# Sample attention of a two-layer decoder step: value products moved next to the following logits, a third key-page buffer, and a later start

## The chip, the core and the metric

The kernel runs on one core of a Trainium2 chip. The metric is device time in microseconds (us) for one launch, from start to end of the program; lower is better. A profiled execution has two times: the device time of that execution, and its span, which runs from the first to the last recorded instruction. Engines are named as in the profile: PE is TensorE's matmul side, PEld its weight loads, DVE is VectorE, ACT is ScalarE, POOL is GpSimd and SP is SyncE, whose queue (SPq) issues all the transfers spoken of here.

## What is computed

One inference step of a two-layer decoder trunk, for a prompt of 1024 tokens and for eight sample sequences of eight tokens each. Layer 0 mixes tokens with gated linear attention. Layer 1 is stick-breaking attention, and the change touches only the sample part of it. Cut to what matters:

```python
def sb_attend(q, k, v, bias, q_offset):
    # z = q.k/sqrt(dh) + bias_h ; key s is read by query t iff s < t
    z = einsum('bqhd,bkhd->bhqk', qi, k) * dh**-0.5 + bias
    valid = k_pos < q_pos
    rest = cumsum(where(valid, log_sigmoid(-z), 0), axis=keys, reverse=True)
    a = exp(where(valid, z + rest, -inf))
    return einsum('bhqk,bkhd->bqhd', a, v)

# samples: 256 past positions in two pages of 128, found through page_table
k_past = gather_pages(cache_k, page_table)      # (8, 256, 16 heads, 64)
v_past = gather_pages(cache_v, page_table)
ys = (sb_attend(q, concat(k_past, k), concat(v_past, v), bias, 256) * silu(g)) @ w_out
```

A page of keys or values of all 16 heads is 128 x 1024 float32, 512 KB; each of the eight sequences reads two of each, so this stage loads 16 MB in 32 transfers.

## The kernel before

The whole kernel is one function. It does not issue its work in the order of its text: every piece is registered with `at(time, function, ...)` and the pieces are then run in the order of these due times. The unit is a *step*: one output tile of a dense product, 24 matmuls of 512 columns in `dense` (helper line L293, where the tile is called acc). The PE engine is the only one whose instructions are kept in exactly this order (`ENGINES` on line 41, `manual_schedule` on line 91). The order of DVE, ACT, POOL and of SP's queue comes from a planner that takes the due order as priority and its own estimate of when things are ready. Each of these queues is executed in order: an instruction that waits holds up all that are behind it.

The end of the program looks like this. `last` is the due time at which prompt attention is over. The output product of layer 1 (16 dense steps for the prompt, two shorter ones for the samples) began about 5.5 steps ahead of `last`; 15 prompt steps come first, then the two sample steps, then the last prompt step. The attention of the eight sample sequences lies between these dense matmuls: its small pieces are put between them on PE, one sequence every `EVERY` = 0.8 of a step. A sequence b has the base time s0 = last + 0.3 + 0.8 b, and its pieces in order are:

- `load_k` (line 1090, due s0 - 0.25): reads the two page numbers into registers and issues the two key pages (L1095) into kp, a tile of two buffers.
- `turn_k` (line 1104, due s0 + 0.5, 0.6, 0.7 and 0.8): four groups of four PE transposes (L1107) that turn the key pages into a bank called tr; ACT copies groups 1 and 3 to KT (L1110), DVE groups 2 and 4 (L1112). There are two tr banks, used in turn by everything that transposes.
- `spread_q` (line 1114, due s0 + 0.6): DVE copies of the queries into QB (L1117).
- `logits_s` (line 1120, due s0 + 1.2): 16 matmuls onto strips of 32 rows of the bank z (L1125), one for the mask (L1127), then two sigmoids on ACT (L1129, L1130).
- `load_v` (line 1098, due s0 + 1.25): issues the two value pages (L1102) into vp, two buffers.
- `stick_s` (line 1132, due s0 + 1.5): a DVE scan (L1135) and a multiply (L1137), which leaves the weights in As.
- `turn_s` (line 1139, due s0 + 1.85): three transposes of As (L1142, L1143), copied by ACT (L1146) and DVE (L1147).
- `weigh_s` (line 1149, due s0 + 2.15): the value products, 24 matmuls onto strips of 32 rows of the bank o (L1154: 16 with the pages vp, 8 with the new rows vs), then two DVE operations (L1157, L1160).
- `turn_o` (line 1162, due s0 + 2.5): one transpose (L1164), copied by DVE (L1166) and then ACT (L1167) into oTs.

When the last sequence is done, `gate_s` (line 1169, due s1 = s0 + 2.75) multiplies by the gate and writes hs (L1170 to L1172), which the first sample matmul needs; it is due at s1 + `S_GAP` at the earliest (line 1201). The residual of a dense step comes from memory into xr (L719), is added on DVE (L725), and goes out (L728).

Of the kernel before, what the change touches and what calls it, by code (L numbers as in the profile page):

```python
# [9 lines left out]
F32 = mybir.dt.float32  # L10
# [7 lines left out]
D = 1024  # L18
# [25 lines left out]
class Timeline:  # L44
# [8 lines left out]
    def at(self, time, fn, *args):  # L53
        assert time >= self.now, (time, self.now)
        heapq.heappush(self.heap, (time, self.n, fn, args))
        self.n += 1
# [20 lines left out]
def tile_hybrid_decoder(ctx, tc, x_prompt, x_sample, state_gla, cache_k, cache_v, page_table,  # L77
# [28 lines left out]

    C_SC, C_T, C_TS = 0.6, 0.9, 2.1
    UNIT0, PACE, L_STICK, L_TURN, L_AV = 1.45, 0.42, 0.26, 0.8, 1.3
    EVERY, S_GAP, TAIL = 0.8, 0.5, 1

    XRING = 3
    NX = {'mid': 3, 'at1': 2, 'sa': 3}
# [3 lines left out]
    at = line.at  # L116
# [11 lines left out]
    def sb(pool, name, shape, dtype=F32, bufs=2, tag=None):  # L128
        return pools[pool].tile(shape, dtype, name=name, tag=tag or name, bufs=bufs)
# [532 lines left out]
    for h in range(GH):  # L662
# [3 lines left out]
        for c, (c_0, n) in enumerate(CH):  # L666
            st = {}
            G.append(st)
            if h == 0:
                a, b = QK0[c]  # L670
                la = LA0[c]
            else:
                a, b = i, i + 1
# [5 lines left out]
            for j, (key, out) in enumerate((("q", q_out), ("k", k_out))):  # L679
                lo, hi = a + (b - a) * 0.5 * j, a + (b - a) * 0.5 * (j + 1)  # L680
                dense_t(lo, hi, c_0, n, wqk,
                        lambda w, k, j=j: (w[k // 2], slice((k % 2) * 256 + j * 128, (k % 2) * 256 + j * 128 + 128)),
# [306 lines left out]
    for p in range(PAIRS):  # L989
# [27 lines left out]
        for m in range(NP // 2):  # L1017
# [10 lines left out]
            for x, (j, c) in enumerate(units):  # L1028
                u = {}
# [14 lines left out]
    last = z0 + L_AV + 0.4  # L1044
# [45 lines left out]
    def load_k(u, b):  # L1090
        u["r"], u["k"] = [], []
        for j in range(2):
            r = nc.sync.value_load(Z["pts"][0:1, 2 * b + j:2 * b + j + 1], min_val=0, max_val=n_phys - 1)
            u["k"].append(sb("sa", "kp", [128, D]))
            nc.sync.dma_start(u["k"][j], ck[bass.ds(r, 1)].rearrange("o p f -> (o p) f"))  # L1095
            u["r"].append(r)

# [75 lines left out]

    at(last, sa_consts)
    for b in range(NB):
        u, s0 = {}, last + 0.3 + EVERY * b
        at(s0 - 0.25, load_k, u, b)
        for j in range(2):
            for g in range(2):
                at(s0 + 0.5 + 0.2 * j + 0.1 * g, turn_k, u, j, g)  # L1180
        at(s0 + 0.6, spread_q, b)
        at(s0 + 1.2, logits_s, u, b)
        at(s0 + 1.25, load_v, u)
        at(s0 + 1.5, stick_s, u)
        at(s0 + 1.85, turn_s, u)
        at(s0 + 2.15, weigh_s, u, b)
        at(s0 + 2.5, turn_o, u, b)
    s1 = s0 + 2.75
    at(s1, gate_s)


# [55 lines left out]
```

## Time and profile before

| | us |
|---|---|
| median of three runs | 1372.65 (1367.76 to 1372.90) |
| the profiled execution, device time | 1375.27 |
| its span | 1373.6 |
| PE busy in the span | 1282.8 (93%) |
| DVE busy | 1012.5 (74%) |
| ACT busy | 709.7 (52%) |
| POOL busy | 587.0 (43%) |
| mean granted clock of PE, as a share of full speed | 0.986 |

PE busy is the sum of the times in which at least one matmul was in the engine; matmuls overlap, so this is not a measure of how well the array is used. Timeline times count from the start of the span. In a timeline row the bracket at the end gives the time for which the engine had been idle before this row, and what released it.

### The profile page before, as it was taken

To read this page: it belongs to the slowest core of one execution; us is meant where nothing else is said; L and a number is where in the kernel's file an instruction comes from. 1 tells how busy PE (TensorE), PEld (TensorE's weight loads), DVE (VectorE), ACT (ScalarE), POOL (GpSimd) and SP (SyncE) were. 2 spreads that over 40 slices of the span, in tenths; PEclk is the share of its full clock that TensorE was granted. 3 is DMA by queue.
4 is the path that set the end of the run, shared out by engine and by line. 5 is a ranking of instruction groups with operands and counts; after the bars stand their busy time and mean duration, and the time that the engine had idled before them with its cause. 6 is when DMAs were issued, how large, how long until landed. Compare 5 with 4: busy or idle time off the path is not lost.

```text
span 1373.6 us, 23656 instructions
## 1 busy us (share of the span) xinstructions
PE 1282.8 (93%) x8025; PEld 1140.3 (83%) x8025; DVE 1012.5 (74%) x2047; ACT 709.7 (52%) x1640; POOL 587.0 (43%) x1101
## 2 busy tenths in 40 slices
PE   6999999999999998989989899898998989989998
PEld 5788888888878788989889898898998988877666
DVE  7858759668564457788888988789788898986443
ACT  6446245352441134566756667566666667763221
POOL 6223223223231216465655846557466574543000
PEclk9999999999999999999999999999999999999999
DMA  6311402304246423020110201102012022134762
GB/s 195 92 32 43 137 20 68 108 32 133 91 129 213 145 101 104 18 81 18 58 42 22 79 17 55 47 24 80 16 41 63 23 89 68 32 121 155 249 245 88
DMA packets 118459, 115.82 MB, mean 84 GB/s; under 512 B 11003, under 2 KB 97923, under 8 KB 118339
## 3 DMA queue, kind: packets, MB, share of 16 engines
q1 hardware_dynamic: 118338, 114.31, 27.2%
q8 instruction: 64, 1.05, 0.3%
q14 instruction: 57, 0.46, 0.1%
HBM read 83.61 MB, written 30.67 MB: 83 GB/s over the span
## 4 chain that ended last, share of the span: by engine, by line
PE 55%; DVE 18%; POOL 9%; ACT 7%; issue 7%; DMA 3%; SPq 1%; POOLq 0%; ACTq 0%; DVEq 0%
PE acc L293 31%; PE acc L315 7%; DVE run L908 4%; PE z L881 3%; PE tr L932 3%; PE o L944 2%; POOL wlo L222 2%; POOL rs L804 2%; ACT qh L853 2%; DVE whi L221 2%; PE o L544 1%; DVE aT L935 1%; DVE wr L217 1%; POOL v L819 1%; PE o L1154 1%
## 5 line engine op out<-in xcount | busy, mean ns | idle before, releaser
L293 PE MATMUL acc<-whi,h 128*128 128x512 f32 (+1 forms) x1728 | 538.7, 374 | 10.1 <-DVE qk L810 7.9
L293 PEld LDWEIGHTS acc<-whi,h 128*128 128x128 f32 x1728 | 313.5, 189 | 41.1 <-ACT sh L954 4.2
L293 PE MATMUL acc<-wlo,h 128*128 128x512 f32 (+1 forms) x864 | 322.5, 373 | 3.9 <-DVE wlo L222 2.5
L315 PE MATMUL acc<-h,whi 128*128 128x256 f32 (+5 forms) x832 | 193.5, 318 | 10.3 <-DVE g L512 5.1
L222 POOL TENSOR_TENSOR wlo<-wr,whi 128x512 fp32r<-128x512 f32 x98 | 139.1, 1422 | 123.5 <-DVE whi L221 93.2
L293 PEld LDWEIGHTS acc<-wlo,h 128*128 128x128 f32 x864 | 162.8, 188 | 22.7 <-DVE wlo L222 3.2
L908 DVE TENSOR_TENSOR_SCAN run<-om,run 128x256 f32<-128x256 f32 x192 | 146.7, 802 | 11.0 <-ACT om L884 10.5
L315 PEld LDWEIGHTS acc<-h,whi 128*128 128x128 f32 (+2 forms) x832 | 141.3, 189 | 15.1 <-DVE g L512 6.0
L934 ACT ACTIVATE aT<-tr 128x512 fp32r<-128x512 f32 (+1 forms) x160 | 88.9, 556 | 103.9 <-PE tr L932 90.2
L884 ACT ACTIVATE om<-z,bias 128x512 f32<-128x512 f32 (+1 forms) x160 | 103.3, 646 | 52.6 <-PE z L881 43.1
L932 PE MATMUL tr<-ident,A 128*128 128x128 f32 x576 | 91.5, 277 | 39.3 <-POOL v L819 18.3
L315 PE MATMUL acc<-h,wlo 128*128 128x256 f32 (+2 forms) x392 | 123.8, 316 | 0.5 <-POOL wlo L222 0.5
L293 PE MATMUL acc<-w,h 128*128 128x384 f32 (+1 forms) x480 | 122.6, 365 | 0.7 <-DVE qk L810 0.7
L932 PEld LDWEIGHTS tr<-ident,A 128*128 128x128 f32 x576 | 69.5, 142 | 55.1 <-POOL run L903 19.4
L935 DVE TENSOR_TENSOR aT<-tr,aT 128x512 fp32r<-128x512 f32 (+1 forms) x160 | 100.8, 630 | 9.1 <-ACT aT L934 6.8
L944 PE MATMUL o<-aT,v 128*128 128x256 f32 x640 | 105.0, 286 | 0.0
L885 ACT ACTIVATE A<-z,bias 128x512 f32<-128x512 f32 (+1 forms) x160 | 102.4, 640 | 0.0
L944 PEld LDWEIGHTS o<-aT,v 128*128 128x128 f32 x640 | 97.2, 194 | 1.8 <-DVE aT L935 1.1
L908 DVE TENSOR_TENSOR_SCAN run<-om 128x128 f32<-128x128 f32 (+1 forms) x128 | 85.0, 695 | 13.6 <-POOL om L890 13.6
L881 PE MATMUL z<-kc,qh 128*128 128x256 f32 x320 | 86.1, 290 | 7.3 <-DVE kc L858 7.3
L804 POOL TENSOR_TENSOR rs<-ms,half_exp 128x4 f32<-128x4 f32 (+1 forms) x72 | 83.9, 1166 | 20.3 <-DVE ms L802 18.8
L293 PEld LDWEIGHTS acc<-w,h 128*128 128x128 f32 x480 | 82.2, 189 | 7.2 <-issue 2.5
(274 smaller groups left out, 2531.7 us busy)
## 6 DMA issues: line engine op xcount, KB each, us to landing
wr<-in_w_in_b_dram SPq DMA_DIRECT2D x64, 256.0 KB, 3.0
wr<-in_w_in_a_dram SPq DMA_DIRECT2D x32, 256.0 KB, 3.2
kp<-in_cache_k_dram SPq DMA_DIRECT2D x16, 512.0 KB, 5.0
vp<-in_cache_v_dram SPq DMA_DIRECT2D x16, 512.0 KB, 4.5
o_d<-og SPq DMA_DIRECT2D x60, 128.0 KB, 1.8
x<-in_x_prompt_dram SPq DMA_DIRECT2D x8, 512.0 KB, 4.8
wr<-in_w_in_a_dram SPq DMA_DIRECT2D x32, 128.0 KB, 3.7
n<-in_state_gla_dram SPq DMA_DIRECT2D x8, 512.0 KB, 3.9
```

The costliest lines, as they stand in the source:

```text
L222: engine.tensor_sub(e.lo[:, :m], raw[:, :m], e.hi[:, :m])
L293: nc.tensor.matmul(st["ps"][:x.shape[1], :n], x, (w[k].hi if part == 0 else w[k].lo)[:, :n], start=first, stop=last)
L315: nc.tensor.matmul(st[key][:x.shape[1], :n], x, y, start=first, stop=last)
L804: nc.gpsimd.tensor_tensor(st["rs"][:n], ms[:n], half_exp[:n], op=OP.pow)
L881: nc.tensor.matmul(out, lhs, rhs, start=x == 0, stop=x == len(mm) - 1)
L884: nc.scalar.activation(u["om"][:, v0:], z[:, v0:], AF.Sigmoid, scale=-1.0, bias=K1["bias"][:, 1, hd:hd + 1])
L885: nc.scalar.activation(u["A"][:, v0:], z[:, v0:], AF.Sigmoid, bias=K1["bias"][:, 0, hd:hd + 1])
L908: nc.vector.tensor_tensor_scan(run[:, a, n - 1::-1], rev, rev, init, op0=OP.mult, op1=OP.bypass)
L932: nc.tensor.transpose(tr[:, x], u["A"][:, col:col + 128], ident)
L934: nc.scalar.activation(hi[:, v0:], tr[:, v0:], AF.Copy)
L935: nc.vector.tensor_sub(lo[:, v0:], tr[:, v0:], hi[:, v0:])
L944: nc.tensor.matmul(q["po"][:, j], vs, part[:, x * 256:(x + 1) * 256], start=first and n == 0, stop=last and n == 3)
```

## The change

It touches constants and due times, and the buffer count of one tile. The base time of every sequence becomes last + 0.9 + 0.8 b. Key pages get three buffers and, except for sequence 0, are due 1.2 steps ahead of the base time (sequence 0: at last + 0.05, as before). Value pages are due at s0 + 0.9, `stick_s` at s0 + 1.3, `turn_s` at s0 + 1.6, and `weigh_s` of sequence b just ahead of the logits of sequence b + 1. The end s1 becomes s0 + 2.6. No matmul, copy or transfer is added or left out.

```diff
-    EVERY, S_GAP, TAIL = 0.8, 0.5, 1
+    S_LAG, EVERY, S_GAP, TAIL = 0.9, 0.8, 0.5, 1
@@ load_k
-            u["k"].append(sb("sa", "kp", [128, D]))
+            u["k"].append(sb("sa", "kp", [128, D], F32, 3))
@@
-        u, s0 = {}, last + 0.3 + EVERY * b
-        at(s0 - 0.25, load_k, u, b)
+        u, s0 = {}, last + S_LAG + EVERY * b
+        at(max(s0 - 1.2, last + 0.05 + 0.01 * b), load_k, u, b)
         for j in range(2):
             for g in range(2):
                 at(s0 + 0.5 + 0.2 * j + 0.1 * g, turn_k, u, j, g)
         at(s0 + 0.6, spread_q, b)
         at(s0 + 1.2, logits_s, u, b)
-        at(s0 + 1.25, load_v, u)
-        at(s0 + 1.5, stick_s, u)
-        at(s0 + 1.85, turn_s, u)
-        at(s0 + 2.15, weigh_s, u, b)
-        at(s0 + 2.5, turn_o, u, b)
-    s1 = s0 + 2.75
+        at(s0 + 0.9, load_v, u)
+        at(s0 + 1.3, stick_s, u)
+        at(s0 + 1.6, turn_s, u)
+
+        at(s0 + 1.2 + EVERY - 0.001, weigh_s, u, b)
+        at(s0 + 2.35, turn_o, u, b)
+    s1 = s0 + 2.6
```

## Rows read from the trace of the kernel before

**Rows 1.** Timeline of PE: the logits of sequences 0 to 3 and 7.

```profile
1266.53 1.28 PE L1125 MATMUL z<-KT,QB 128*32 128x320 f32 x16
...
1275.54 1.28 PE L1125 MATMUL z<-KT,QB 128*32 128x320 f32 x16
...
1288.82 1.28 PE L1125 MATMUL z<-KT,QB 128*32 128x320 f32 x16
...
1298.49 1.28 PE L1125 MATMUL z<-KT,QB 128*32 128x320 f32 x16
...
1338.25 1.28 PE L1125 MATMUL z<-KT,QB 128*32 128x320 f32 x16
```

**Rows 2.** Waits of PE from 1251 us on (total, times, longest); timeline rows of two.

```profile
PE tr L1107 <- DMA kp<-in_cache_k_dram: 3.8, 4, 1.8
...
PE tr L1107 <- DVE KT L1112: 0.5, 1, 0.5
...
1279.33 0.63 PE L1107 MATMUL tr<-ident,kp 128*128 128x128 f32 x4 [1.82 <-DMA kp<-in_cache_k_dram]
...
1330.25 0.63 PE L1107 MATMUL tr<-ident,kp 128*128 128x128 f32 x4 [0.61 <-ACT As L1130]
```

**Rows 3.** Windows: busy time of PE, PEld, DVE, ACT, POOL; clock, DMA share, GB/s.

```profile
1266.50:1275.50 9.00, 8.10 (x56) 5.68 (x55) 3.96 (x8) 2.53 (x5) 1.30 (x2) 1.00 0.96 335
...
1281.00:1282.00 1.00, 1.00 (x12) 0.40 (x8) 0.00 (x0) 0.00 (x0) 0.00 (x0) 0.50 0.00 0
```

**Rows 4.** Timeline of PE: value products of sequence 2, and dense rows around such pieces.

```profile
1290.98 0.71 PE L293 MATMUL acc<-w,h 128*128 128x512 f32 x2
1291.62 1.07 PE L1154 MATMUL o<-vp,aTs 128*32 128x256 f32 x16
...
1293.75 0.71 PE L293 MATMUL acc<-w,h 128*128 128x512 f32 x2
1294.30 0.60 PE L1107 MATMUL tr<-ident,kp 128*128 128x128 f32 x4
...
1301.29 1.07 PE L1154 MATMUL o<-vp,aTs 128*32 128x256 f32 x16
1302.17 0.61 PE L1154 MATMUL o<-vs,aTs 128*32 128x256 f32 x8
1302.72 0.50 PE L293 MATMUL acc<-w,h 128*128 128x512 f32 x1
...
1352.72 4.24 PE L293 MATMUL acc<-w,h 128*128 128x512 f32 x18
```

**Rows 5.** Timelines of ACT and PE: how long a tr bank is held.

```profile
1294.99 0.60 ACT L1110 ACTIVATE KT<-tr 128x512 f32<-128x512 f32 x1 [3.07 <-PE tr L1107]
1297.08 0.22 ACT L1167 ACTIVATE oTs<-tr 64x64 f32<-64x64 f32 x1 [1.49 <-DVE oTs L1166]
...
1296.34 0.27 PE L1164 MATMUL tr<-ident,os 128*64 128x128 f32 x1
```

**Rows 6.** Timelines of PE and DVE: from the end of sequence 3's logits to its weights.

```profile
1299.71 0.20 PE L1127 MATMUL z<-wmask,identb 128*128 128x64 bf16 x1
...
1301.53 0.49 DVE L1137 TENSOR_TENSOR As<-As,runs 128x320 f32<-128x320 f32 x1
```

**Rows 7.** Timeline of SP's queue, and the landing time of the key pages (tile view).

```profile
1281.46 1.19 SPq L1102 DMA_DIRECT2D vp<-in_cache_v_dram  x2
...
1294.02 2.37 SPq L1095 DMA_DIRECT2D kp<-in_cache_k_dram  x2
...
1323.96 1.39 SPq L1095 DMA_DIRECT2D kp<-in_cache_k_dram  x2
...
DMA to landing us min/median/max: 3.4/5.0/6.2
```

**Rows 8.** Timelines of PE and DVE: from the last sequence's turn to hs.

```profile
1350.54 0.27 PE L1164 MATMUL tr<-ident,os 128*64 128x128 f32 x1
...
1352.73 0.69 DVE L1172 TENSOR_TENSOR hs<-oTs,hs 128x512 fp32r<-128x512 f32 x1
```

## The prediction, made before the changed kernel was run

> **What bounds the kernel now.** The order of reading was: the page's busy times, PE's waits in the stretch that the change touches, the timeline of that stretch, and then the other queues there. On the page PE is the engine with the most work, 93% of the span, and PE keeps its order exactly as written. So what the change can win or lose is time in which PE stands, or runs at a lower clock, between `last` (about 1254 us) and the end. The amount of PE work is the same.
>
> The simplest yardstick is the distance from one sequence's logits to the next. Undisturbed, from sequence 2 to sequence 3, it is 1298.49 - 1288.82 = 9.67 us [rows 1]: 0.8 of a step of dense matmuls, four groups of key transposes, one set of logits, one of value products, two small transposes. From sequence 1 to 2 it is 13.28 us, 3.6 us more. Of this, 1.82 us is the wait for sequence 2's first key page [rows 2]; the other 1.8 us is PE's clock, which was granted at 0.50, the 1.2 GHz level, after that wait [rows 3]. All waits of PE in this stretch add up to 3.8 us in four waits for key pages, 0.6 us in one that the profile puts down to ACT, and 0.5 us for a tr bank that DVE had not copied [rows 2]. The 0.6 us is a key page too, I think: sequence 7's first page was issued in the pair that began at 1323.96 [rows 7] and the wait ends at 1330.25 [rows 2]; a landing of 6.2 us, the longest in rows 7, gives 1330.2. So what the stretch loses today is 3.8 + 0.6 + 0.5 + 1.8 = 6.7 us, 0.5% of the run. That is nearly the ceiling of the change, and 0.5% (6.9 us) is about what a measurement of this kernel can tell from no change.
>
> **The later start.** Sequence 0's key pages are due at last + 0.05 before and after, but their first transposes go from last + 0.8 to last + 1.4. A dense matmul takes 4.24 us / 18, less the tail of the last one, about 0.23 us [rows 4]; 0.6 of a step is 14.4 of them, 3.3 us. Two of the four key-page waits are sequence 0's, and no wait is longer than 1.8 [rows 2], so 3.3 us covers them. The start later costs nothing by itself: dense matmuls that stood behind the sample work now stand ahead of it, until they run out. They don't: the 15 prompt steps end 9.5 steps after `last`, and the gate is due at last + 0.9 + 5.6 + 2.6 = 9.1. What is left behind the last `turn_o` (due at 8.85) is 0.66 of a step, 16 matmuls, 3.6 us. The chain from that transpose to hs took 1352.73 + 0.69 - 1350.54 = 2.9 us, with an unrelated DVE addition in it [rows 8]. It fits, with 0.7 us to spare; cost 0. That the earliest due time of the samples (9.6) now passes the 9.5 only leaves a hole in due times and none on PE.
>
> **Three key buffers.** With two, both pages of the next sequence wait until this one's have been turned. In the steady stretch the pair for sequence 4 is issued from 1294.02, at the end of sequence 3's second group of transposes (its third starts at 1294.30 [rows 4, 7]), and sequence 4's first group comes right after sequence 3's logits, which began at 1298.49, so near 1300.5. That is 6.5 us ahead, against a landing time of 5.0 median and 6.2 longest [rows 7]; so little slack is why a busy moment on SP or on the DMA engines (share 0.96 between sequences 0 and 1 [rows 3]) shows up on PE. With three, page n takes the buffer of page n - 3. The first page of a sequence is then free to load almost two periods ahead (some 16 us), the second about one (9.7 us and half a microsecond more). Both exceed 6.2. I take all 4.4 us of waits, 3.8 and 0.6, as gone; the bounds are 4.4 and 2 (if the planner leaves the issues in SP's queue where they are, the later start still saves sequence 0's and helps sequence 1's). The 1.8 us of low clock should go with the 1.82 us wait in front of it: bounds 1.8 and 0, and I take 1.8, because sequences 2 to 7, without such a wait, keep to about 9.9 us on average [rows 1]. The 0.5 us for the tr bank belongs to DVE's backlog at the start of the stage, where it still casts weights; I leave it, bounds 0.5 gained and 2 lost: an addition on DVE that waits for its residual could now stand between two key copies.
>
> **Value products directly in front of logits.** Now they are separated by dense matmuls, so PE goes in and out of work on 32-column strips twice per sequence. Going in: two dense matmuls after a transpose take 0.64 us up to value products (1290.98 to 1291.62) and 0.55 up to a transpose (1293.75 to 1294.30), 0.09 more. Going out: the 8 last value matmuls take 0.55 (1302.17 to 1302.72), while 16 take 0.88 (1301.29 to 1302.17), so 8 should take 0.44; 0.11 more [rows 4]. Seven pairs merge (value products 0 to 6 with logits 1 to 7): 7 x 0.2 = 1.4 us at most and 0 at least, since the trace has no logits directly after value products. The nearest row, the step from vp to vs at an unchanged pace, speaks for most of it; I take 1.2. The Trainium skill, on the page "TensorEngine Tiling (Array Packing)", section "Key Properties", states that changing the tiling mode drains TensorE while changing the tile does not; the rows' 0.09 and 0.11 us agree with a drain on each side, and by that rule the sum would take 1.4 here instead of 1.2.
>
> **What becomes tighter.** `weigh_s` moves behind `turn_s`, so the small transposes crowd together: after sequence b's logits come three groups of key transposes, `turn_o` of b - 1, then the fourth group and `turn_s` of b, all in 0.4 of a step, and six uses of two banks. A bank with a key group is held from 1294.30 [rows 4] to 1294.99 + 0.60 [rows 5], 1.29 us from its first transpose. The third group's bank is wanted again after 2.4 dense matmuls (0.55), the group itself (0.60 to its last result [rows 4], of which the next matmul overlaps some 0.2) and `turn_o` (about 0.1), so 1.1 us later: 0.2 short. `turn_o`'s bank is held from 1296.34 to 1297.08 + 0.22, 0.96 us [rows 5], and is wanted about as late: 0 to 0.1 short. Six sequences (1 to 6) have all of this: 6 x 0.3 = 1.8 us lost; bounds 0 and 3.6, the latter where ACT reaches the copy 0.3 late.
>
> From logits to `turn_s` only 0.4 of a step is left instead of 0.65. As is ready 1301.53 + 0.49 - 1299.71 = 2.3 us after the mask matmul [rows 6]. Sequences 0 to 6 have 9.6 dense matmuls (2.2 us) and three or four key groups in between, so it is hidden; sequence 7 has no key groups behind it, 2.2 against 2.3: 0.1 lost. From `turn_s` to `weigh_s` it is again 2.2 us, against about a microsecond for ACT's and DVE's copies; 0. Moving `stick_s` earlier by due time changes nothing, DVE does it when the sigmoid is there. `load_v` still waits for the value products two pages back, whatever its due time, and has a whole period less those products, about 8 us, to land: 0.
>
> **The sum.** Gained 4.4 + 1.8 + 1.2 = 7.4; lost 1.8 + 0.1 = 1.9; net 5.5 us. Against the profiled execution: 1375.27 - 5.5 = 1369.8 (span 1368.1). That execution lay 2.6 us above the median of the three runs, so the forecast for the median is 1372.65 - 5.5 = 1367.2. The bounds: at best 4.4 + 1.8 + 0.5 + 1.4 with nothing lost, 8.1, gives 1364.6; at worst 2 + 0 + 0 - 3.6 - 0.1 - 2 = -3.7, so 1376.3, if everything goes wrong at once.
>
> **Rivals.** (A) *The waits go and no bank runs short.* ACT's copy starts a little earlier or the planner's order fits: 8.1 us, 1364.6. For it: the two banks are short by only 0.2 us on paper. Against: six uses in 0.4 of a step, all in ACT's and DVE's in-order queues.
>
> (B) *The gain is given back in the stage's first 25 us.* The DMA engines are 0.96 busy there [rows 3], and three key pages asked for early push back the first value pages and the residuals that DVE's additions wait for; DVE then holds key copies, and PE stands as long as before. About 1372.6. For it: today that stretch is full. Against: the start is 3.3 us later with the same bytes.
>
> (C) *Slower: SP's queue.* By due time the key pages of sequence b + 2 (s0 + 0.4 of b) now stand ahead of the value pages of b (s0 + 0.9); before, they stood behind them (1.35 and 1.25). If the planner keeps that order in the queue, the value pages can't be issued until the second group of b + 1 has been turned, which frees the second key page's buffer: about 2.3 us after logits b (4.8 dense matmuls, two groups). Value products b start 9.67 - 1.43 - 1.22 = 7.0 us after these logits (durations from rows 1, 4 and 6). The second page then has 4.1 us, and needs 5.0 to 6.2: 0.9 to 2.1 late, and the logits behind the value products wait too. Seven times 1.5 is 10.5, plus one more dip of the clock, 2; less the 5.5: 1379.7, and 1384 with the longest landing. It decides as soon as the lead falls under the landing time. For it: the queue is in order, and today SP already reaches value loads early and sits there. Against: today's planner issues key pages the moment that they are free [rows 7], so it seems to order by readiness, and by readiness the value pages come first.
>
> **Chances.** The forecast, 0.50; A, 0.27; B, 0.13; C, 0.10. Faster by over 0.5% (under 1365.8) is most of A and a little of the forecast: 0.30. Slower by over 0.5% (over 1379.5) is most of C: 0.08. Between: 0.62. The range from 1363.0 to 1375.5 takes in A, B and all but the last of the bounds, with some microsecond of spread; C is left out.
>
> **What would show it.** In the trace after: no waits of PE for kp beyond 0.3 us in all, no clock of 0.50 between sequences 1 and 2, logits 0.8 of a step apart at 9.6 to 9.9 us throughout; logits directly after value products with no added gap; short waits of the fourth key group or of `turn_s` for ACT, 0.2 to 0.3 us per sequence. If instead PE's value products wait for vp, C holds; if PE waits for DVE's KT copies near sequence 0, B does. The forecast is wrong if the period of the middle sequences is itself above 10 us.

## The result: slower, because the value pages now stand behind waiting key pages in SP's queue

The changed kernel takes 1381.04 us (median of five runs, 1379.20 to 1383.76) against 1372.05 before (five runs, 1367.76 to 1372.90): a ratio of 1.0079, with a 95% interval from 1.0058 to 1.0100 (the ratio is not that of the two medians, which is 1.0066). The forecast was 1367.2 and a gain; the outcome is the third rival, to which the prediction gave one chance in ten and a time of 1379.7.

The first view to read is PE's waits from 1245 us on (total, times, longest), which answers to [rows 2]:

```profile
PE o L1154 <- DMA vp<-in_cache_v_dram: 12.0, 11, 3.2
PE tr L1107 <- ACT KT L1110: 0.2, 1, 0.2
PE tr L1142 <- ACT KT L1110: 0.2, 1, 0.2
```

The key pages, for which PE waited four times before, are gone from the list. In their place stands a wait that the kernel before did not have: the value products wait 12.0 us for their pages. PE's timeline shows what that does to the distance of one sequence's logits from the next ([rows 1]):

```profile
1264.86 1.28 PE L1125 MATMUL z<-KT,QB 128*32 128x320 f32 x16
...
1276.04 1.08 PE L1154 MATMUL o<-vp,aTs 128*32 128x256 f32 x8 [3.24 <-DMA vp<-in_cache_v_dram]
1277.70 1.08 PE L1154 MATMUL o<-vp,aTs 128*32 128x256 f32 x8 [0.58 <-DMA vp<-in_cache_v_dram]
1278.56 1.08 PE L1154 MATMUL o<-vs,aTs 128*32 128x256 f32 x8
1279.41 2.36 PE L1125 MATMUL z<-KT,QB 128*32 128x320 f32 x16
...
1283.77 0.60 PE L1107 MATMUL tr<-ident,kp 128*128 128x128 f32 x4
...
1291.04 0.64 PE L1154 MATMUL o<-vp,aTs 128*32 128x256 f32 x8 [1.98 <-DMA vp<-in_cache_v_dram]
...
1293.44 2.38 PE L1125 MATMUL z<-KT,QB 128*32 128x320 f32 x16
...
1351.66 1.26 PE L1125 MATMUL z<-KT,QB 128*32 128x320 f32 x16
```

The first two distances are 14.55 us and 14.03 us, and the average from sequence 0 to sequence 7 is 12.4 us (86.80 / 7). Before, the undisturbed distance was 9.67 us and the average 10.2 ((1338.25 - 1266.53) / 7, [rows 1]). Two costs are seen in these rows: the wait itself in the brackets, and logits that last 2.36 us instead of 1.28, because the clock had fallen.

Why the pages are late is told by SP's queue. Its timeline around the value pages of sequence 1, and SP's own waits in the whole stretch:

```profile
1284.40 0.35 SPq L1095 DMA_DIRECT2D kp<-in_cache_k_dram  x1
1285.27 0.88 SPq L1102 DMA_DIRECT2D vp<-in_cache_v_dram  x2
```

```profile
SPq L1095 <- PE tr L1107: 23.0, 8, 8.1
...
SPq L1102 <- PE o L1154: 1.9, 4, 0.7
```

The value pages' buffers were free when the value products of sequence 0 had read them: the rows that begin at 1276.04 and 1277.70 are the last readers, and the new rows vs follow at 1278.56. But the queue issued the pages only at 1285.27, 6.7 us later. Just ahead of them stands a key page (the second of sequence 3), whose buffer is released by sequence 2's second group of transposes, at 1283.77 plus 0.60; it goes out at 1284.40, and only then the queue reaches the value pages. PE starts on them 5.8 us after their issue, as soon as they have landed. Before, they had 10.2 us, from 1281.46 [rows 7] to 1291.62 [rows 4]. SP's waits have changed places accordingly: before, SP stood 16.2 us at value loads (waiting for value products) and 7.4 at key loads; now 1.9 and 23.0. SP's waits in the kernel before:

```profile
SPq L1102 <- PE o L1154: 16.2, 9, 5.4
SPq L1095 <- PE tr L1107: 7.4, 9, 1.5
```

Sequence 0 differs in one point. Its value pages stand behind sequence 2's second key page as well, but they were also slow to land:

```profile
1268.41 0.35 SPq L1095 DMA_DIRECT2D kp<-in_cache_k_dram  x1
...
1269.43 0.89 SPq L1102 DMA_DIRECT2D vp<-in_cache_v_dram  x2
```

PE could read them 6.6 us (first page, at 1276.04) and 7.7 us (second, at 1277.70) after their issue; the median over all value pages is 5.1, and the DMA engines' share was 1.00 from 1272.60 to 1276.04. So some 1.5 us of the longest wait, 3.24 us, is landing time and not the queue.

### The profile page after: what moved, and what is told of

It reads as the page before. It is cut to its first block, busy times and chain, and to the rows that moved or that the text cites. A ratio compares the mean times of both kernels' runs of the same rounds, so it can differ in the third digit from the quotient of the medians.

```text
span 1382.1 us, 23648 instructions
## 1 busy us (share of the span) xinstructions
PE 1282.4 (93%) x8025; PEld 1139.6 (82%) x8025; DVE 1012.3 (73%) x2047; ACT 708.8 (51%) x1640; POOL 589.7 (43%) x1101
## 3 DMA queue, kind: packets, MB, share of 16 engines
q8 instruction: 64, 1.05, 0.3%
## 4 chain that ended last, share of the span: by engine, by line
PE 55%; DVE 17%; POOL 8%; ACT 7%; DMA 5%; issue 5%; SPq 1%; POOLq 0%; ACTq 0%; DVEq 0%
PE acc L293 32%; PE acc L315 7%; DVE run L908 4%; PE z L881 3%; DMA vp<-in_cache_v_dram 3%; PE tr L932 3%; PE o L944 3%; POOL wlo L222 2%; POOL rs L804 2%; ACT qh L853 2%; DVE whi L221 2%; PE o L544 1%; DVE wr L217 1%; DVE aT L935 1%; POOL v L819 1%
```

## Experiments

The theory is that the order in SP's in-order queue is the whole harm, and that the due times set this order. Two rivals: that key and value pages in flight together slow each other down on the DMA engines, and that the value products are simply placed too early. All ratios below are to the kernel before, measured on the same chip, with 95% intervals. Differences in us from the changed kernel are differences of medians that were not measured together: the median of the kernel before moved by up to 1.4 us (1370.80 to 1372.22) from one such measurement to another.

**Value pages first, by the key pages' due time.**

```diff
-        at(max(s0 - 1.2, last + 0.05 + 0.01 * b), load_k, u, b)
+        at(max(s0 - 0.6, last + 0.05 + 0.01 * b), load_k, u, b)
```

> The changed kernel with one due time altered: key pages are due 0.6 of a step ahead of a sequence's base time instead of 1.2, so that the value pages of sequence b (base + 0.9) come before the key pages of b + 2 (base + 1.0) in SP's queue. Three key buffers, the later start and the value products next to the logits stay. Theory 1 (queue order): the value pages were late because they stood behind a key page that waits for transposes; here PE's waits for vp fall from 12.0 us to under 2, the three dips of the clock go, and the time falls from 1381 to about 1367 (the sum of the prediction). Theory 2 (transfers): three key pages in flight slow down the value pages; those transfers are the same here, so PE still waits for vp some 8 to 12 us and the time stays above 1377. Theory 3 (the value products are placed too early): the same, above 1377.

1364.16 us, ratio 0.9943 (0.9922 to 0.9964). PE's waits in that stretch:

```profile
PE tr L1107 <- DMA kp<-in_cache_k_dram: 1.0, 1, 1.0
PE tr L1142 <- ACT KT L1110: 0.2, 1, 0.2
PE tr L1107 <- ACT KT L1110: 0.2, 1, 0.2
```

No wait for a value page is left, with the same buffers, the same transfers and the same places on PE. One due time is worth 16.9 us by the medians (18.6 by the ratios, (1.0079 - 0.9943) x 1371), and with it the change is a gain. The median landing time of a value page is 5.3 us here and 5.1 in the changed kernel, so these pages don't land faster; they are issued earlier. That speaks against both rivals.

**Two key buffers, with the changed due times.**

```diff
-            u["k"].append(sb("sa", "kp", [128, D], F32, 3))
+            u["k"].append(sb("sa", "kp", [128, D]))
```

> The changed kernel with key pages in two buffers again, all due times as changed. Theory 1 (queue order): both key pages of b + 2 now stand ahead of the value pages of b and wait for the fourth group of transposes of b + 1 instead of the second, 0.2 of a step plus two groups later (about 2 us); each of six or seven waits for vp grows by 1 to 2 us, so slower than the changed kernel, 1386 to 1396. Theory 2 (transfers): with at most two key pages in flight the value pages land earlier, so faster than the changed kernel, 1372 to 1378.

1405.15 us, ratio 1.0236 (1.0209 to 1.0263): worse than either theory said, and in the direction of the queue. PE's first wait, and SP's:

```profile
PE o L1154 <- DMA vp<-in_cache_v_dram: 24.3, 8, 4.9
```

```profile
SPq L1095 <- PE tr L1107: 42.0, 7, 11.0
```

With two buffers the key pages ahead of the value pages wait for a later group of transposes, and PE's waits double from 12.0 to 24.3 us. Fewer pages in flight did not help: the value pages landed in 5.1 us (median) as before. The waits grew by 12.3 us, which is within what was expected. The size was missed since only the waits were priced and not the clock: of the six logits behind such a wait five last 2.36 us, and PE busy, from the logits of sequence 0 to those of sequence 7, is 83.35 us against 74.18 in the changed kernel, for the same 561 instructions.

**The later start alone,** on the kernel before.

```diff
-        u, s0 = {}, last + 0.3 + EVERY * b
-        at(s0 - 0.25, load_k, u, b)
+        u, s0 = {}, last + 0.9 + EVERY * b
+        at(s0 - 0.25 if b else last + 0.05, load_k, u, b)
```

> The kernel before with one part of the change: base time last + 0.9 instead of last + 0.3; sequence 0's key pages stay at last + 0.05, everything else moves along. Two key buffers, old order of value products and logits. The prediction's step: sequence 0 has 3.3 us more for its pages, so its two waits go (1.1 us) and perhaps the 0.5 for a tr bank; sequences 1 and 2 may keep theirs (0.9 and 1.8, with a dip of the clock of 1.8). Expected 1367 to 1371. If the later start itself costs (a gate chain that no longer fits at the end), 1373 or more.

1368.59 us, ratio 0.9977 (0.9964 to 0.9990): some 3 us gained, as expected, and no cost at the end. PE's waits are 1.7 us for key pages in three and 0.5 in one put down to ACT, all of them behind sequence 0:

```profile
PE tr L1107 <- DMA kp<-in_cache_k_dram: 1.7, 3, 0.8
PE tr L1107 <- ACT As L1130: 0.5, 1, 0.5
```

**The value products next to the logits alone,** on the kernel before.

```diff
-        at(s0 + 1.5, stick_s, u)
-        at(s0 + 1.85, turn_s, u)
-        at(s0 + 2.15, weigh_s, u, b)
-        at(s0 + 2.5, turn_o, u, b)
-    s1 = s0 + 2.75
+        at(s0 + 1.3, stick_s, u)
+        at(s0 + 1.6, turn_s, u)
+        at(s0 + 1.2 + EVERY - 0.001, weigh_s, u, b)
+        at(s0 + 2.35, turn_o, u, b)
+    s1 = s0 + 2.6
```

> The kernel before with one part of the change: value products of sequence b directly ahead of the logits of b + 1, with the due times of the weights' scan and transposes and of the output turn as changed; base time, key and value loads and two key buffers as before. The prediction's step: 0.20 us saved in each of seven pairs (1.4) less 0.2 to 0.3 us of tr-bank waits in six sequences (1.8), so within 2 us of before, 1370 to 1374, with value products followed by logits without a gap. Theory 3 (the place of the value products is the harm): PE waits for vp here too, above 1377.

1367.97 us, ratio 0.9977 (0.9962 to 0.9992), better than expected. PE's waits:

```profile
PE tr L1107 <- DMA kp<-in_cache_k_dram: 1.7, 4, 0.7
PE tr L1107 <- DVE KT L1112: 0.6, 1, 0.6
PE tr L1142 <- ACT KT L1110: 0.3, 2, 0.2
PE tr L1107 <- ACT KT L1110: 0.2, 1, 0.2
```

No value page is waited for, so the place of the value products does no harm by itself. Why the key-page waits are down from 3.8 to 1.7 us as well was not pursued; the planner's order on SP differs a little in this kernel too.

**The third key buffer alone,** on the kernel before: the one-line change of the tile, `F32, 3`.

> The kernel before with one part of the change: key pages in three buffers, all due times as before. In SP's queue the value pages of b stand ahead of the key pages of b + 2, as before. The prediction's step: the third buffer lets the first page of a pair go early, so the key-page waits of sequences 1, 2 and 7 (0.9, 1.8, 0.6) and the dip of the clock (1.8) go; sequence 0's 1.1 us stays. Expected 1366 to 1369. If the third buffer is worth nothing by itself (the issue times are set by SP and not by the buffer), 1370 to 1372.

1371.52 us, ratio 0.9996 (0.9982 to 1.0009): nothing. PE's waits:

```profile
PE tr L1107 <- DMA kp<-in_cache_k_dram: 2.0, 4, 0.8
PE tr L1107 <- DVE KT L1112: 1.1, 2, 0.7
PE tr L1107 <- ACT As L1130: 0.6, 1, 0.6
```

Waits for key pages remain (2.0 us), now with a median landing time of 6.4 us instead of 5.0 [rows 7], and DVE's copies hold PE longer. The queue gets to the key pages no earlier, since value pages that wait for value products stand in front of them: sequence 4's first key page is issued at 1289.84, 6.0 us ahead of its transposes at 1295.79, where it had 6.5 us before. A buffer that is free earlier helped nothing here without an earlier issue.

**Value pages first, by their own due time.**

```diff
-        at(s0 + 0.9, load_v, u)
+        at(s0 + 0.35, load_v, u)
```

> The changed kernel with one due time altered, and another one than in the first experiment: value pages are due at base + 0.35 instead of base + 0.9, which puts them ahead of the key pages of b + 2 (due at base + 0.4). Key pages keep their early due times. Theory 1 (the order in SP's queue is the whole harm, and the due times set it): PE's waits for vp under 2 us, 1362 to 1367, like the first experiment. Theory 4 (early key loads do harm by themselves, by what they push back): slower than the first experiment by over 3 us, 1368 to 1378.

1362.25 us, ratio 0.9937 (0.9918 to 0.9956), the best of all and 18.8 us under the changed kernel. Key pages keep their early due times, so these do no harm either. In its trace PE waits for no page at all. SP and PE around the value pages of sequence 1:

```profile
1272.40 0.34 SPq L1102 DMA_DIRECT2D vp<-in_cache_v_dram  x1
...
1273.46 0.34 SPq L1102 DMA_DIRECT2D vp<-in_cache_v_dram  x1
1274.01 0.97 SPq L1095 DMA_DIRECT2D kp<-in_cache_k_dram  x1
```

```profile
1272.43 1.26 PE L1125 MATMUL z<-KT,QB 128*32 128x320 f32 x16
...
1280.56 1.07 PE L1154 MATMUL o<-vp,aTs 128*32 128x256 f32 x16
1281.45 0.61 PE L1154 MATMUL o<-vs,aTs 128*32 128x256 f32 x8
1281.88 1.26 PE L1125 MATMUL z<-KT,QB 128*32 128x320 f32 x16
```

The value pages go out as the logits of sequence 1 begin (1272.43), with 7 to 8 us until they are needed at 1280.56; in the changed kernel they went out 5.9 us after these logits began, and PE could start on them only 11.6 us after them.

The same stretch in both kernels, from the logits of sequence 0 to those of sequence 7, holds the same PE instructions, 561 of them. The windows (columns as in [rows 3]) split the 19.86 us between them. First the changed kernel, with one window in which the clock was low; then this one:

```profile
1279.40:1281.70 2.30, 2.30 (x20) 0.60 (x13) 1.03 (x2) 0.00 (x0) 0.20 (x1) 0.50 0.44 120
...
1264.86:1351.66 86.80, 74.18 (x561) 48.12 (x564) 34.88 (x74) 18.97 (x41) 2.91 (x14) 0.92 0.61 209
```

```profile
1263.24:1330.18 66.94, 66.50 (x561) 46.61 (x564) 35.00 (x74) 18.96 (x41) 2.91 (x14) 1.00 0.76 271
```

PE idle is 86.80 - 74.18 = 12.6 us against 0.4: the waits. PE busy is 74.18 against 66.50 for the same instructions, 7.7 us more. Most of that is the lower clock, 0.92 on average against 1.00: in windows of half a microsecond it stands at 0.50 for 13.7 us in all, 12.7 of them with PE busy, so some 6.4 us is slower work (an estimate: half of 12.7). The rest, 1.3 us, is about what the split value products add, since two halves of 8 matmuls are counted at 0.64 us each where 16 together take 1.07.

**Value pages first, and sequence 0's key pages back at last + 0.05.**

```diff
-        at(max(s0 - 1.2, last + 0.05 + 0.01 * b), load_k, u, b)
+        at(s0 - 0.6 if b else last + 0.05, load_k, u, b)
```

> The first experiment's kernel with sequence 0's key pages due at last + 0.05 again (there they had slipped to last + 0.3, and a weight load came between the two pages; PE waited 1.0 us for a key page). That wait goes: 1.0 us less than the first experiment, 1362 to 1364.5. If the wait comes from the DMA engines and not from the issue time, the same as the first experiment.

1363.26 us, ratio 0.9938 (0.9919 to 0.9958). The 1.0 us wait is gone from the trace; the medians differ by 0.9 us, in the expected direction, but the intervals overlap.

**The change without the new place of the value products.** Due times of `stick_s`, `turn_s`, `weigh_s`, `turn_o` and s1 back at their old offsets, the rest as changed.

> The changed kernel without its title part: scan, small transposes, value products, output turn and end at their old offsets from the base time (1.5, 1.85, 2.15, 2.5, 2.75); later start, three key buffers and the due times of both kinds of loads as changed. Theory 1 (queue order): the value pages still stand behind a key page, but the value products now come 0.15 of a step and the next sequence's logits later, some 2 us, so PE's waits for vp fall to about half or less, 1370 to 1377. Theory 3 (the place next to the logits is the harm): no waits for vp at all, 1366 to 1369.

1370.38 us, ratio 0.9992 (0.9978 to 1.0006). PE's waits:

```profile
PE o L1154 <- DMA vp<-in_cache_v_dram: 3.0, 5, 1.0
```

The value pages are issued as late as in the changed kernel (those of sequence 1 at 1282.07, 7.8 us after its logits began at 1274.26; in the changed kernel 5.9), but they are needed 0.15 of a step, the next logits and some transposes later, and the wait falls from 12.0 to 3.0 us. So the place next to the logits is not the cause by itself, as it makes no such wait alone; but it used up the slack that would have hidden most of the late issue. The order in the queue is not the whole harm either: the loss against the kernel before needs both. Here the gain of the other parts and the remaining wait about cancel.

**Start and place as changed, loads as before:** two buffers, key pages due at s0 - 0.25 (sequence 0's at last + 0.05), value pages at s0 + 1.25.

> The change without its loads: base time last + 0.9 and value products next to the logits as changed, but two key buffers and the old due times of both kinds of loads (key pages at base - 0.25, sequence 0's at last + 0.05, value pages at base + 1.25), so that value pages stand ahead of the key pages that they used to stand ahead of. It asks what the third buffer and the early key pages are worth beside the other two parts. If the key pages' slack of about 1 us is enough once the start is later: within 2 us of the kernels with three buffers and value pages first, 1362 to 1365. If the third buffer is needed: waits for kp of 2 to 4 us, 1365 to 1369.

1364.64 us, ratio 0.9946 (0.9931 to 0.9961), and one wait for a page, 0.5 us for a key page. The two other parts carry most of the gain; what the third buffer and the early key pages add (0.9937 against 0.9946) is within the intervals.

**Value pages from another queue.** All due times and buffers as changed.

```diff
-            nc.sync.dma_start(u["v"][j], cv[bass.ds(u["r"][j], 1)]...)
+            r = nc.scalar.value_load(Z["pts"][...])
+            nc.scalar.dma_start(u["v"][j], cv[bass.ds(r, 1)]...)
```

> The changed kernel with all due times and buffers as they are; only the value pages are issued from ACT's queue instead of SP's, with the page numbers read into ACT's registers. Key pages stay on SP and wait there as before. Theory 1 (the value pages are late because they stand behind a waiting key page in one in-order queue): PE's waits for vp fall under 2 us and the time to 1361 to 1368, a little above the best one because ACT spends some 1 to 2 us per sequence on register reads and issues. Theory 2 (transfers are slow when key and value pages are in flight together): PE still waits for vp, over 1375.

1364.95 us, ratio 0.9941 (0.9928 to 0.9955). PE's waits:

```profile
PE tr L1108 <- DMA kp<-in_cache_k_dram: 1.4, 2, 0.9
PE tr L1143 <- ACT KT L1111: 0.2, 1, 0.2
PE tr L1108 <- ACT KT L1111: 0.2, 1, 0.2
```

This takes away the standing behind: key pages still wait on SP (15.0 us for their transposes), the due times, buffers and bytes are the same, and the waits for value pages are gone. One thing moves besides: sequence 0's value pages go out at 1252.44, far ahead of their due time. The Trainium skill, page "DMA: Bandwidth & Descriptors", section "Issuing engines are not separate DMA queues", states that issuing from several engines only saves the time that it takes to initiate a transfer, which is usually small. Here it saved 16.1 us by the medians, although the transfers landed no faster (median 5.1 us in both): what was saved is the time that an issue stood behind another one's wait, and for that the measurement decides.

## Why the prediction was wrong, point by point

*What bounds the stretch.* Right: PE's idle time and its clock decide. Rightly ordered, the change gains 8.6 us (0.63% of 1371, from the ratio 0.9937), above the 6.7 us of losses and close to the 8.1 of rival A.

*The later start.* Right: sequence 0's waits went, the end held, and alone it is worth 3 us.

*Three key buffers.* The waits for key pages did go, all 3.8 us of them, in the changed kernel. But the reason was not the third buffer: alone it gains nothing. With two buffers, the later start alone leaves 1.7 us of waits for key pages (and 0.5 put down to ACT), the new place of the value products alone leaves 1.7 as well, and the two together leave 0.5. That step credited the buffer with what start and place do together; why the place helps is open. The dip of the clock that the sum counted as 1.8 us to be gained was in the profiled execution. The kernels with a single part of the change have no such dip in their traces (granted clock 1.00 from 1250 to 1356 us in all three), and the third buffer alone has no gain in its median. The sum took losses off the median that it had read in an execution 2.6 us above it. That execution's mean granted clock was 0.986; in 23 executions of the kernel before that ran beside the experiments it went from 0.985 to 0.995 and tended to be higher in the shorter ones (0.995 at 1366.75 us, 0.985 at 1376.17). So the term was probably worth less than 1.8 us in the median; how much stays open.

*Value products in front of logits.* Right, and the larger bound: in the fast kernel 8 value matmuls take 1281.88 - 1281.45 = 0.43 us up to the logits, where they took 0.55 up to a dense matmul [rows 4], so neither drain is left between the two. The rule of the Trainium skill's page "TensorEngine Tiling (Array Packing)", section "Key Properties", that only a change of the tiling mode drains, agrees with these 0.43 us.

*The crowded transposes.* The mechanism is there, waits for ACT's copy of key groups, but in the whole stretch there are two of them, 0.16 and 0.17 us, in the changed kernel and with the value pages first alike; the sum charged 0.3 six times.

*The step that failed* is the one sentence on `load_v`: that it "still waits for the value products two pages back, whatever its due time", at a cost of 0. It looked at what the load itself waits for and not at what stands ahead of it. The runs showed in its place 12.0 us of waits for value pages: those of sequence 1 were issued 6.7 us after their buffers were free, behind a key page that waited for its own buffer. The same due times were read rightly in rival C, with the right place (behind the key page that waits for the second group), the right lead (4.1 us on paper; for sequence 1, 5.8 measured from the issue to PE's start, 1.98 of them waited for, so 3.8), and nearly the right time: 1379.7 against 1381.04. What kept its chance at 0.10 was the argument that the planner orders by readiness. The row behind it, key pages issued the moment that they are free, is what one sees under either rule, since in the steady stretch of the kernel before due order and ready order are the same. It could not tell them apart, and should have left the chance near even. Another row of the kernel before speaks for due order:

```profile
1267.49 0.34 SPq L1095 DMA_DIRECT2D kp<-in_cache_k_dram  x1
1268.03 0.86 SPq L1102 DMA_DIRECT2D vp<-in_cache_v_dram  x2
```

These value pages are sequence 0's, whose buffers no earlier value product holds, and the key page in front is sequence 1's second, whose buffer was held until sequence 0's fourth group of transposes at 1263.66. By readiness the value pages would have come first. It is one row; the two experiments that move only a due time show that among SP's loads due time decides.

*The price.* Rival C had seven waits of 1.5 us and one dip of the clock. Measured: 12.0 us of waits in sequences 0 to 5 and none in 6 and 7, where no key pages are left to stand behind (sequence 0 was not in the price: its value pages had free buffers all along, and stood behind sequence 2's second key page); and low clock at three places, some 6.4 us of slower work where 2 were charged. The gain of the rest came out larger than 5.5 (8.6 where the order is right), which hid part of this in the total: that C's time came within 1.4 us is partly luck.

## What to carry to other kernels

When a load's due time is moved past another load's on the same in-order queue, price the wait of whichever now stands in front as if the one behind had it too: compare the moment at which each buffer is released, not only the moment at which each page is wanted. A row of the kernel before can only say which rule a planner follows if the two rules would give different rows. And a transfer that is late need not be a slow transfer: look at its issue time before its landing time.

## What was not expected of the hardware

In the changed kernel the granted clock fell to 0.50, the 1.2 GHz level, at three places: during the wait of 3.24 us in front of sequence 0's value products; at the end of sequence 1's value products, which had waited 1.98 and 0.53 us; and at the end of sequence 5's, which had waited 1.05 and 0.75 us. It did not fall after the 0.16 and 1.75 us of sequence 4, so the longest wait alone does not tell whether it falls:

```profile
1328.16 0.64 PE L1154 MATMUL o<-vp,aTs 128*32 128x256 f32 x8 [1.75 <-DMA vp<-in_cache_v_dram]
...
1329.05 1.26 PE L1125 MATMUL z<-KT,QB 128*32 128x320 f32 x16
...
1339.69 0.64 PE L1154 MATMUL o<-vp,aTs 128*32 128x256 f32 x8 [0.75 <-DMA vp<-in_cache_v_dram]
...
1340.61 2.38 PE L1125 MATMUL z<-KT,QB 128*32 128x320 f32 x16
```

Each time the low clock lasted over the logits (2.36 to 2.38 us for logits that take 1.26 at the 2.4 GHz level). It made the waits cost over half as much again: some 6.4 us of slower work beside 12.0 us of waits.
